# Low-part products last in each branch column tile, and a larger readiness margin for two early steps of a hybrid attention and retention layer

## The chip, the cores and the metric

The kernel runs on one core of a Trainium2 chip. The metric is the device time of one execution in microseconds (us); the times below are medians of several executions. The engines are named as in the profile: PE is TensorE (matmuls; PEld its weight loads), DVE is VectorE, ACT is ScalarE, POOL is GpSimd, and SP is the queue that issues the DMAs of this kernel. A trailing q (PEq) means the engine's sequencer.

## The reference

One layer of a streaming encoder is applied to 2048 new frames (the prompt) and to 64 frames of a running stream (the sample), which has 4096 frames of cached keys and values.

```
h = rmsnorm(x, norm_g) @ w_in            # 1024 -> 6144 columns
qa, ka, va, za, qb, kb, vb, zb, ga, gb = split(h)
qa, ka = rmsnorm over each 64 of qa, ka  # 4 heads, two 64-wide halves
oa = softmax(q0 k0) v - lam * softmax(q1 k1) v    # differential attention, ALiBi, chunk mask
ob = retention(qb, kb, vb)                        # per-head decay, chunks of 64
oa = rmsnorm(oa) * 0.8 * silu(za)
ob = rmsnorm(ob) * silu(zb)
m = sigmoid(ga) * (oa @ w_oa) + sigmoid(gb) * (ob @ w_ob)
y = x + m @ w_out
```

The outputs are y, the normalised keys, the values and the retention states, for the prompt and for the sample. All is float32. TensorE is given operands in a reduced float32 type, so each operand is split into a high part (rounded) and a low part (what is left), and a product is three matmuls: high by high, high by low and low by high.

## The kernel before, in words

**One order for all engines, written by a planner.** The program is unrolled in Python. TensorE, ACT and DVE carry out their instructions in just the order in which the generator writes them (their schedule is manual). That order comes from a list scheduler in the kernel itself: class Hybrid keeps a clock for each engine (`self.pe`, `self.act`, `self.dve`, `self.pool`, `self.dma`); P, A, V and G (L258 to L272) add the cost that the planner assumes for one instruction and return the time when its result is taken to be there (250 ns behind its end). Work is cut into generator tasks with priorities. A task yields the planner time at which it wants to go on; `loop` (L197) resumes the task of the best priority whose time has come on TensorE's clock, and if there is none, moves that clock forward. So a `yield t` puts other tasks' matmuls ahead of what follows; what is written then waits on the chip by semaphores for its true inputs. Two margins that are added to such times matter here: SLACK is 400 ns and LAND is 2000 ns.

**Stages.** First the prompt's first 1024 rows and the sample's 64 rows go through the input projection (wide pieces of 512 columns, `natural`, then Strassen-like products, `strassen`), and beside them the sample's attention runs (`sample_attn`, `sample_pv`). Then the second 1024 rows are scaled and split (`x_scaled`, `x_split`, L494 and L540) and projected, with the prompt's attention heads and the retention beside it. Last come the branch projections (`out_stream`, `m_tile`) and the output projection (`y_quad`).

**Key and query rows, `fin_qk` (L1289).** For each 128 rows of a key or query piece: ACT squares the PSUM bank, DVE reduces and scales, a small reciprocal root follows, DVE writes the normalised rows `raw` (L1325), the planner time t of which is given SLACK more (L1326) and yielded. Behind it come the store of the rows to the key output (keys only), four transposes on PE (L1340), the split of the result on ACT and DVE into a high and a low part (L1350 to L1356), and their stores to the DRAM scratch kT or qT. `t0` is the first row of the tile; it is 0 only for the first tile of the prompt, once for the keys and once for the queries. The buffers are `ev` (3), `tlo` (2) and `thi` (1).

**The sample's probabilities times values, `sample_pv` (L2209).** For each of 4 heads, 5 tiles of probabilities: PE transposes them (L2273) into a bank, ACT rounds (L2287) and DVE subtracts (L2289), which makes the pieces `atp`; there are two pieces per tile (one in the last), nine per head. A piece is entered in `parts` with its planner time plus 500 ns (L2291). The inner function `mms` (L2252) yields until the later of that time and of the time of the split values `vhl` (two buffers, filled by `v_split`: ACT L2186, DVE L2189), then writes four matmuls (L2258). The products of one tile are written after the transposes of the next. The heads' result is folded at L2135; `x_scaled` waits for it.

**Branch column tiles, `m_tile` (L2654).** For each group g of 264 columns (256 prompt rows and 8 sample rows), branch br and column tile ct of 128 there is one accumulation over four 128-row slices kt of the branch width. `self.wo[br][kp]` holds the weights' high and low parts (wh, wl), and `og[kp]` the gated branch's (ogh, ogl), two slices in one tile; `og_fin` (L2609) makes them, ogh on ACT (L2627) and ogl on DVE (L2630), and enters them with 700 ns of margin. For each kt three matmuls are written: wh by the high part (L2673), wh by the low part (L2674), wl by the high part (L2675). `m_fin` (L2681) then multiplies the bank by the gate on DVE (L2686) and adds the branches (L2698).

Of the kernel before, what the change touches and what calls it, by code (L numbers as in the profile page):

```python
# [27 lines left out]
GW = 264  # L28
# [12 lines left out]
SLACK = 400.0  # L41
PACE = 700.0
LATE = 1000.0
LAND = 2000.0
# [128 lines left out]
class Hybrid:  # L173
# [1115 lines left out]
    def fin_qk(self, which, g, nh=2):  # L1289
        nc = self.nc  # L1290
        ep = self.ep
        hs = slice(2 * g, 2 * g + nh)

        def fin(ps, r, nu, t0, t, bank="mm"):
            n, ng, rt = 128 * nh * nu, 2 * nh * nu, r * nu
            yield from self.take("ev")
            yield from self.take("tlo")
            raw = self.sb(ep, [128, 512], "ev", "raw")[:r, :n]
            sq = self.sb(ep, [128, 512], "tlo", "sq")[:r, :n]
            ms = self.sp.tile([128, 8], F32, tag="ms", name="ms")[:r, :ng]  # L1300
            raw3 = raw.rearrange("p (g d) -> p g d", d=64)
            nc.scalar.activation(sq, ps, AF.Square)
            t1 = self.A(n, t)
            if which == "q":
                nc.scalar.copy(raw, ps)
                t2 = self.A(n, t)
            else:
                nc.vector.tensor_mul(raw3, ps.rearrange("p (g d) -> p g d", d=64),  # L1308
                                     self.gk[:r].unsqueeze(1).to_broadcast([r, ng, 64]))
                t2 = self.V(n, t)  # L1310
            self.give(bank, max(t1, t2))
            yield t1
            nc.vector.tensor_reduce(ms, sq.rearrange("p (g d) -> p g d", d=64),
                                    axis=AX.X, op=ALU.add)
            t = self.V(n, t1)
            self.give("tlo", t)
            if which == "q":
                nc.vector.scalar_tensor_tensor(out=ms, in0=ms, scalar=64.0 * EPS,
                                               in1=self.qinv[:r, 2 if nh == 4 else g, :ng], op0=ALU.add, op1=ALU.mult)
            else:  # L1320
                nc.vector.tensor_scalar(ms, ms, 1.0 / 64, EPS, op0=ALU.mult, op1=ALU.add)
            t = self.V(80)
            yield t
            rs = yield from self.rsqrt_small(ms, ng, t)
            nc.vector.tensor_mul(raw3, raw3, rs.unsqueeze(2).to_broadcast([r, ng, 64]))  # L1325
            t = self.V(n + 100) + SLACK  # L1326
            yield t
            ts = 0
            if which == "k":
                if t0 < T:  # L1330
                    dst = self.o["k_prompt"][0, 0, t0:t0 + rt, hs]
                else:
                    dst = self.o["k_sample"][0, 0, :, hs]
                ts = self.rows_out(dst.rearrange("t h c d -> t (h c d)"), raw, nu, nh << 16)
            yield from self.take("tp")
            tp = self.psum("tp")
            for u in range(nu):
                for h in range(nh):
                    c = 128 * (nh * u + h)
                    nc.tensor.transpose(tp[:, h * rt + u * r:h * rt + u * r + r], raw[:, c:c + 128],  # L1340
                                        self.ident[:r, :r])
                    t = self.P(256)
            self.give("ev", max(t, ts))
            yield from self.take("thi")
            yield from self.take("tlo")
            hi = self.sb(ep, [128, 512], "thi", dt=F32R)[:, :nh * rt]
            lo = self.sb(ep, [128, 512], "tlo", dt=F32R)[:, :nh * rt]
            pt = tp[:, :nh * rt]
            if which == "q":
                nc.scalar.activation(hi, pt, AF.Identity, scale=self.gq)  # L1350
                nc.vector.scalar_tensor_tensor(out=lo, in0=pt, scalar=self.gq, in1=hi.bitcast(F32),
                                               op0=ALU.mult, op1=ALU.subtract)
                dst = self.qT
            else:
                nc.scalar.copy(hi, pt)
                nc.vector.tensor_sub(lo, pt, hi.bitcast(F32))  # L1356
                dst = self.kT
            t1 = self.A(n, t, 40)
            t2 = self.V(n, t1)
            self.give("tp", t2)  # L1360
            for d, s, tag, w in zip(dst, (hi, lo), ("thi", "tlo"), (t1, t2)):
                if w > self.pe:
                    yield w
                self.give(tag, self.st(d[hs, :, t0:t0 + rt].rearrange("h p t -> p h t"),
                                       s.bitcast(F32).rearrange("p (h t) -> p h t", h=nh), nh * nu << 16))
            if t0 == T:
                self.fresh.add(which)

        return fin
# [839 lines left out]
    def sample_pv(self, h, units, tail, tt, te, lp, oall, moved):  # L2209
# [3 lines left out]
        nc = self.nc  # L2213
# [8 lines left out]
        for _ in range(3):  # L2222
            t = self.V(9, te[-1])
        yield t
        yield from self.take("s")
        ps = self.psum("s")
        nc.tensor.matmul(ps[:, 0:2], self.fold, l, start=True, stop=True)
        t = self.P(512)
# [5 lines left out]
        for _ in range(3):  # L2234
            t = self.V(100, t)
# [30 lines left out]
        for m in range(5):  # L2266
            nt, r = (4, 128) if m < 4 else (1, 64)
            yield tb[m // 2]
            yield from self.take("at")
            at = self.psum("at")  # L2270
            for k in range(nt):
                src = units[m // 2][:, (m % 2) * 512 + 128 * k:(m % 2) * 512 + 128 * k + 128] if m < 4 else tt
                nc.tensor.transpose(at[:r, r * k:r * k + r], src, self.ident[:r, :r])  # L2273
                t = self.P(256)
            if m == 1 or m == 3:
                self.drop(units[m // 2], t)
            tags = ("ath", "atl") if m < 4 else ("ath",)
            if todo is not None and not self.has(*tags):
                yield from mms(*todo)
                todo = None  # L2280
            parts = []
            for k, tag in enumerate(tags):
                yield from self.take(tag)
                a = self.sb(ap, [128, 512], tag, "atp", F32R)
                c = at[:r, :128 * nt].rearrange("p (k c q) -> p k c q", c=2, q=64)[:, :, k]
                s = a[:r, :128 * nt].rearrange("p (k c q) -> p k c q", c=2, q=64)
                nc.scalar.copy(s[:, :, 0], c)  # L2287
                t2 = self.A(64 * nt, t)
                nc.vector.tensor_sub(s[:, :, 1], c, s[:, :, 0].bitcast(F32))  # L2289
                t2 = self.V(64 * nt, t2)  # L2290
                parts.append((a, tag, t2 + 500))  # L2291
            self.give("at", t2)
            yield self.pe
            if todo is not None:
                yield from mms(*todo)
            todo = (m, nt, r, parts)
        yield from mms(*todo)
        t = done[0]
        yield t
        oh = oall[:, 128 * h:128 * h + 128]  # L2300
        nc.scalar.activation(oh, pv[:, 0:128], AF.Identity, scale=num)
        t = self.A(128, t, 90)
# [351 lines left out]
    def m_tile(self, g, br, ct, second, og):  # L2654
        nc = self.nc
        csl = slice(128 * ct, 128 * ct + 128)
        self.nbank += 1
        tag = ("mm", "s", "at", "mm", "s", "at", "pv", "tp")[self.nbank % 8]
        yield from self.take(tag)
        ps = self.psum(tag)[:, :GW]  # L2660
        for kt in range(4):
            kp, u = divmod(kt, 2)
            wh, wl, tw = self.wo[br][kp]
            yield lambda: ct // 2 in tw
            ready = tw[ct // 2]
            if u == 0 and len(og) == kp:
                yield lambda: self.ogs[g, br, kp]
                og.append(self.ogs[g, br, kp][0])
                ready = max(ready, og[-1][2])
            if ready > self.pe:  # L2670
                yield ready
            oh, ol = (o[:, GW * u:GW * u + GW] for o in og[kp][:2])
            nc.tensor.matmul(ps, wh[:, u, csl], oh, start=kt == 0, stop=False)  # L2673
            nc.tensor.matmul(ps, wh[:, u, csl], ol, start=False, stop=False)  # L2674
            nc.tensor.matmul(ps, wl[:, u, csl], oh, start=False, stop=kt == 3)  # L2675
            for _ in range(3):
                t = self.P(GW)
        self.spawn(self.m_fin(g, br, ct, second, ps, tag, t), 0)
        yield self.pe

# [526 lines left out]
```

## Time and profile before

| what | value |
|---|---|
| median of 3 runs | 1882.4 us (1882.38 to 1887.38) |
| profiled execution, its own time | 1886.05 us |
| span of the profiled execution | 1883.4 us |
| instructions in it | 33013 |
| granted TensorE clock | 1.0 throughout |
| DMA moved | 340.07 MB, mean 181 GB/s |

The span runs from the first to the last instruction of one execution; the difference to its own time lies before and after. In the list of waits a row names the instruction that waited, who released it, the total in us, the number of times and the longest. In a timeline row stand the start and the duration in us, the engine, the line, the operation, the tiles (out<-in), the shape, a count where like instructions are merged (the duration then reaches from the first start to the last end), and in square brackets the engine's idle time before it and who ended it. A matmul's duration is modelled and longer than the step from one matmul to the next, since they are pipelined; steps are read from start to start. In the view of a line or a tile a row has the shortest, median and longest duration in ns and the first and last start in us.

### The profile page before, as it was taken

To read this page: it belongs to the slowest core of one execution; us is meant where nothing else is said; L and a number is where in the kernel's file an instruction comes from. 1 tells how busy PE (TensorE), PEld (TensorE's weight loads), DVE (VectorE), ACT (ScalarE), POOL (GpSimd) and SP (SyncE) were. 2 spreads that over 40 slices of the span, in tenths; PEclk is the share of its full clock that TensorE was granted. 3 is DMA by queue.
4 is the path that set the end of the run, shared out by engine and by line. 5 is a ranking of instruction groups with operands and counts; after the bars stand their busy time and mean duration, and the time that the engine had idled before them with its cause. 6 is when DMAs were issued, how large, how long until landed. Compare 5 with 4: busy or idle time off the path is not lost.

```text
span 1883.4 us, 33013 instructions
## 1 busy us (share of the span) xinstructions
PE 1866.8 (99%) x11090; PEld 1644.6 (87%) x11090; DVE 1328.1 (71%) x3112; ACT 975.3 (52%) x2266; POOL 678.6 (36%) x728
## 2 busy tenths in 40 slices
PE   9999999999999999999999999999999999999999
PEld 7788878888888789888988889899999999998887
DVE  6765856658585678787587877777876769887664
ACT  6444545554434566555455655556666446654221
POOL 2420366555552122122210344253224555532442
PEclk9999999999999999999999999999999999999999
DMA  7654555666767967565523659446437988886552
GB/s 255 216 175 123 161 166 169 176 200 198 240 189 186 253 198 190 152 174 169 145 72 101 172 136 238 129 123 154 126 109 234 259 250 255 263 257 211 165 157 78
DMA packets 402555, 340.07 MB, mean 181 GB/s; under 512 B 85329, under 2 KB 348625, under 8 KB 401362
## 3 DMA queue, kind: packets, MB, share of 16 engines
q1 hardware_dynamic: 402386, 337.97, 61.8%
q8 instruction: 87, 1.43, 0.3%
q14 instruction: 82, 0.67, 0.1%
HBM read 218.27 MB, written 118.75 MB: 179 GB/s over the span
## 4 chain that ended last, share of the span: by engine, by line
PE 82%; DMA 7%; DVE 5%; ACT 2%; SPq 2%; issue 1%; POOL 1%; DVEq 0%; ACTq 0%; POOLq 0%
PE mm L1137 27%; PE mm L989 8%; PE tp L989 4%; PE at L1992 3%; PE s L1880 2%; PE s L1881 2%; PE s L989 2%; PE pv L1972 2%; PE pv L1971 2%; PE pv L1970 2%; DMA ws<-in_w_in_dram 2%; PE s L2799 1%; PE s L2798 1%; PE s L2797 1%; SPq L280 1%
## 5 line engine op out<-in xcount | busy, mean ns | idle before, releaser
L748 POOL TENSOR_TENSOR wl<-ws,wh 128x512 fp32r<-128x512 f32 x107 | 148.9, 1402 | 256.4 <-ACT wh L727 181.5
L1137 PE MATMUL mm<-wh,xh 128*128 128x512 f32 x504 | 203.0, 403 | 0.0
L1137 PE MATMUL mm<-wh,xl 128*128 128x512 f32 x504 | 198.2, 393 | 0.0
L1137 PE MATMUL mm<-wl,xh 128*128 128x512 f32 x504 | 198.0, 393 | 0.1
L1137 PE MATMUL mm<-xh,wh 128*128 128x288 f32 (+2 forms) x544 | 179.8, 330 | 0.0
L1137 PE MATMUL mm<-xh,wl 128*128 128x288 f32 (+2 forms) x544 | 175.6, 323 | 0.0
L1137 PE MATMUL mm<-xl,wh 128*128 128x288 f32 (+2 forms) x544 | 175.5, 323 | 0.0
L1920 ACT ACTIVATE row<-row,a_mx 128x1024 f32<-128x1024 f32 (+7 forms) x144 | 149.8, 1042 | 11.9 <-DVE a_mx L1899 11.9
L2008 DVE TENSOR_TENSOR atl<-at,ath 128x512 fp32r<-128x512 f32 (+1 forms) x144 | 92.6, 658 | 76.6 <-ACT ath L2006 76.3
L2006 ACT CAST ath<-at 128x512 fp32r<-128x512 f32 (+1 forms) x144 | 79.1, 564 | 106.6 <-PE at L1992 106.0
L856 POOL TENSOR_TENSOR wl<-ws,wh 128x256 fp32r<-128x256 f32 x64 | 54.8, 856 | 199.0 <-ACT wh L847 198.9
L1747 POOL TENSOR_TENSOR r_y<-r_y,r_sq 128x256 f32<-128x256 f32 x32 | 28.3, 884 | 238.2 <-DVE r_sq L1744 154.5
L1137 PEld LDWEIGHTS mm<-wh,xl 128*128 128x128 f32 x504 | 94.6, 188 | 21.5
L1137 PEld LDWEIGHTS mm<-wl,xh 128*128 128x128 f32 x504 | 95.0, 188 | 18.5 <-POOL wl L748 0.9
L1137 PEld LDWEIGHTS mm<-wh,xh 128*128 128x128 f32 x504 | 94.8, 188 | 17.8 <-DVE raw L1308 0.2
L1137 PEld LDWEIGHTS mm<-xh,wh 128*128 128x128 f32 x544 | 102.4, 188 | 7.2
L1137 PEld LDWEIGHTS mm<-xl,wh 128*128 128x128 f32 x544 | 102.5, 188 | 6.9
L1137 PEld LDWEIGHTS mm<-xh,wl 128*128 128x128 f32 x544 | 102.3, 188 | 6.6
L1889 DVE CUSTOM_DVE_ANT_0 row<-s,dfar 128x512 f32<-128x512 f32 (+2 forms) x141 | 87.1, 629 | 23.8 <-PE s L1881 18.0
L1942 DVE SCALAR_TENSOR_TENSOR row<-row,a_w 128x1024 f32<-128x1024 f32 (+5 forms) x88 | 96.9, 1106 | 0.0
L1880 PE MATMUL s<-K,q 128*128 128x512 f32 (+3 forms) x240 | 90.5, 378 | 1.2 <-DVE a_acc L1889 1.2
L727 ACT CAST wh<-ws 128x512 fp32r<-128x512 f32 x111 | 67.7, 620 | 41.4 <-DMA ws<-in_w_in_dram 12.7
(543 smaller groups left out, 6075.4 us busy)
## 6 DMA issues: line engine op xcount, KB each, us to landing
ws<-in_w_in_dram SPq DMA_DIRECT2D x155, 256.0 KB, 3.5
q<-qT SPq DMA_DIRECT2D x128, 128.0 KB, 3.9
K<-kT SPq DMA_DIRECT2D x48, 256.0 KB, 4.7
V<-vN SPq DMA_DIRECT2D x24, 512.0 KB, 5.9
row<-in_x_prompt_dram SPq DMA_DIRECT2D x16, 512.0 KB, 4.6
wz<-in_w_in_dram SPq DMA_DIRECT2D x32, 256.0 KB, 4.3
row<-in_cache_k_T_dram SPq DMA_DIRECT2D x32, 256.0 KB, 3.2
row<-in_cache_v_diff_dram SPq DMA_DIRECT2D x32, 256.0 KB, 3.8
```

What stands on the lines that cost most here:

```text
L727: self.nc.scalar.copy(h, st)
L748: eng.tensor_sub(l, st, h.bitcast(F32))
L856: nc.gpsimd.tensor_sub(l[:, cs], src, h[:, cs].bitcast(F32))
L989: nc.tensor.matmul(ps, w[:, c], xs[x][c], start=bool(tag) and c == 0 and i == 0, stop=c == 3 and i == 2, skip_group_check=True)
L1137: nc.tensor.matmul(ps, p, q, start=c == 0 and i == 0, stop=c == KC - 1 and i == 2)
L1880: nc.tensor.matmul(ps, q1s, kk, start=True, stop=False)
L1889: nc.vector.tensor_tensor_reduce(out=row[:, k0:k0 + n], in0=ps, in1=tab, scale=-SLOPES[h], scalar=3.0e38, op0=ALU.add, op1=ALU.min, accum_ ...
L1920: nc.scalar.activation(u, u, AF.Exp, bias=mx, scale=-1.0, accum_out=lp[:, k:k + 1])
L1942: nc.vector.scalar_tensor_tensor(out=u0, in0=u1, scalar=w[:, 0:1], in1=u0, op0=ALU.mult, op1=ALU.add)
L1992: nc.tensor.transpose(at[:, w:w + 128], src, self.ident)
L2006: nc.scalar.copy(ah[:, :w], at[:, :w])
L2008: nc.vector.tensor_sub(al[:, :w], at[:, :w], ah[:, :w].bitcast(F32))
```

## The change

Three places are edited. In `fin_qk` the margin behind the normalised rows becomes LAND (2000 ns) in place of SLACK (400 ns) for the tile with t0 == 0. In `sample_pv` the margin of each piece becomes LAND in place of 500 ns. In `m_tile` the twelve matmuls of a tile are written in another order: for each kt the two products with the high part of the gated branch, and after all four kt the four products with its low part; the last of these now closes the accumulation. The number of matmuls and their operands stay the same.

```diff
@@ -1323,7 +1323,7 @@
             yield t
             rs = yield from self.rsqrt_small(ms, ng, t)
             nc.vector.tensor_mul(raw3, raw3, rs.unsqueeze(2).to_broadcast([r, ng, 64]))
-            t = self.V(n + 100) + SLACK
+            t = self.V(n + 100) + (LAND if t0 == 0 else SLACK)
             yield t
             ts = 0
             if which == "k":
@@ -2288,7 +2288,7 @@
                 t2 = self.A(64 * nt, t)
                 nc.vector.tensor_sub(s[:, :, 1], c, s[:, :, 0].bitcast(F32))
                 t2 = self.V(64 * nt, t2)
-                parts.append((a, tag, t2 + 500))
+                parts.append((a, tag, t2 + LAND))
             self.give("at", t2)
             yield self.pe
             if todo is not None:
@@ -2669,12 +2669,16 @@
                 ready = max(ready, og[-1][2])
             if ready > self.pe:
                 yield ready
-            oh, ol = (o[:, GW * u:GW * u + GW] for o in og[kp][:2])
+            oh = og[kp][0][:, GW * u:GW * u + GW]
             nc.tensor.matmul(ps, wh[:, u, csl], oh, start=kt == 0, stop=False)
-            nc.tensor.matmul(ps, wh[:, u, csl], ol, start=False, stop=False)
-            nc.tensor.matmul(ps, wl[:, u, csl], oh, start=False, stop=kt == 3)
-            for _ in range(3):
-                t = self.P(GW)
+            nc.tensor.matmul(ps, wl[:, u, csl], oh, start=False, stop=False)
+            for _ in range(2):
+                self.P(GW)
+        for kt in range(4):
+            kp, u = divmod(kt, 2)
+            nc.tensor.matmul(ps, self.wo[br][kp][0][:, u, csl], og[kp][1][:, GW * u:GW * u + GW],
+                             start=False, stop=kt == 3)
+            t = self.P(GW)
         self.spawn(self.m_fin(g, br, ct, second, ps, tag, t), 0)
         yield self.pe
```

## The prediction

> **What bounds the kernel now.** I began with the page's busy times, went on to the list of who TensorE waited for, and from there to the timeline around the three places that the change touches.
>
> ```profile
> span 1883.4 us, 33013 instructions
> ...
> PE 1866.8 (99%) x11090; PEld 1644.6 (87%) x11090; DVE 1328.1 (71%) x3112; ACT 975.3 (52%) x2266; POOL 678.6 (36%) x728
> ```
> ```profile
> PE at L2674 <- DVE ogl L2630: 1.9, 4, 1.0
> PE pv L1970 <- ACT ath L2006: 1.6, 1, 1.6
> PE tp L1880 <- DMA q<-qT: 1.4, 1, 1.4
> PE s L1880 <- DVE a_acc L1889: 1.2, 1, 1.2
> PE tp L1340 <- DVE raw L1325: 1.1, 1, 1.1
> ...
> PE pv L2258 <- DVE atp L2289: 0.9, 1, 0.9
> ```
>
> TensorE sets the end: 1883.4 - 1866.8 = 16.6 us are left in which it does not work, and no instruction of it is added or taken away by this change. So a gain can only come out of those 16.6 us (and the slower restart behind a wait, which counts as busy), while a loss has no such ceiling. Three of the six waits shown stand at lines that the change touches: 1.9 at L2674 (branch tiles), 1.1 at L1340 (transposes of a key tile), 0.9 at L2258 (the sample's probabilities times values): 3.9 us. The other three are in places that the edits do not name.
>
> **The first key tile.** The 400 ns of margin become 2000, so 1.6 us more in the planner's clock before the four transposes are written into TensorE's order.
>
> ```profile
> 82.77 0.40 PE L1137 MATMUL mm<-wl,xh 128*128 128x512 f32 x1
> 83.01 0.40 PE L1137 MATMUL mm<-wh,xl 128*128 128x512 f32 x1
> 84.50 0.66 PE L1340 MATMUL tp<-ident,raw 128*128 128x128 f32 x4 [1.09 <-DVE raw L1325]
> ```
> ```profile
> 83.75 0.69 DVE L1325 TENSOR_TENSOR raw<-raw,sm_y 128x512 f32<-128x512 f32 x1
> ```
>
> A projection matmul of 512 columns starts 0.24 us after the one before (82.77, 83.01), so the transposes could have started at 83.25 and started at 84.50: 1.25 us lost, of which 1.09 is plain idling. A projection yields after every six matmuls, 1.4 us; 1.6 us of margin moves the transposes by one or two such groups, to 84.7 or 86.1, when the tile (ready at 83.75 + 0.69 = 84.44) is there. Gain 1.2 (1.1 to 1.3). Moved with them: the store of the key tile on the SP queue, the ACT copy and the DVE subtraction that split it, and the two stores of the parts. The second key tile takes the next of three evacuation buffers, and its matmuls are what TensorE runs meanwhile; were no buffer free, it would wait at most the same 1.6 us. The stored parts are read back only by the attention heads, a stage later. The first query tile moves alike: only one wait is listed at L1340, so there is nothing to gain there and, with projections behind it, nothing to lose.
>
> **The sample's weights.** The margin on each split piece of the transposed probabilities grows from 500 to 2000 ns: 1.5 us in 36 pieces (nine per head).
>
> ```profile
> 280.32 0.40 PE L989 MATMUL mm<-S1h,wl 128*128 128x512 f32 x1
> 281.64 1.60 PE L2258 MATMUL pv<-vhl,atp 128*128 128x256 f32 x8 [0.92 <-DVE atp L2289]
> ...
> 289.77 1.14 PE L2258 MATMUL pv<-vhl,atp 128*128 128x256 f32 x8
> ```
> ```profile
> 432.55 1.61 PE L2258 MATMUL pv<-vhl,atp 128*128 128x256 f32 x8
> ```
> ```profile
> 281.18 0.41 DVE L2289 TENSOR_TENSOR atp<-at,atp 128x256 fp32r<-128x256 f32 x1
> 282.02 0.42 DVE L2289 TENSOR_TENSOR atp<-at,atp 128x256 fp32r<-128x256 f32 x1 [0.44 <-ACT atp L2287]
> 282.90 0.42 DVE L2289 TENSOR_TENSOR atp<-at,atp 128x256 fp32r<-128x256 f32 x1 [0.46 <-ACT atp L2287]
> ...
> 288.27 1.84 DVE L2189 TENSOR_TENSOR vhl<-row,vhl 128x512 fp32r<-128x512 f32 x2
> ```
>
> The first piece was ready at 281.59 and used at 281.64: 281.64 - (280.32 + 0.24) = 1.08 us lost. The eight matmuls of its first two pieces then took 1.60 where an unhindered eight took 1.14: 0.46 more; the same eight in another head took 1.61: 0.47. Sum 2.0, lower bound the 0.9 of the wait list. With 1.5 us more, six projection matmuls fit in between. I take 1.8 (0.9 to 2.0), near the top, since the readiness of both pieces falls inside the new margin. What this does to the sample's own chain: the third piece was ready at 282.90 + 0.42 = 283.32 and used only at 289.77, directly behind the split of its values (288.27 to 290.11 for two). So past the first two pieces the values decide, not the pieces, and the larger margin is hidden by them: a head is late by about 1.5 us, not nine times that, and four heads by at most 6 us. The loads of later values on the SP queue and their splits on ACT and DVE, released by the products, slip by the same 1.5. Behind the sample wait the scaling of the next 1024 rows and their splits:
>
> ```profile
> L2135 PE MATMUL pv<-fold,row x8: 218/275/275, 528.0 to 528.8; 128*128 128x64 f32 x8
> ```
> ```profile
> L528 DVE SCALAR_TENSOR_TENSOR row<-row,gT,rb x24: 472/953/1058, 544.7 to 566.2; 128x256 f32<-128x256 f32 x24
> ```
> ```profile
> L561 ACT CAST xh<-xT x4: 620/622/625, 580.0 to 582.1; 128x512 fp32r<-128x512 f32 x4
> ```
>
> The scaling ends at 566.2 + 0.95 = 567.2; the first split, which needs the first half's input tiles to be done with, starts at 580.0. That is 12.8 us of cover for at most 6 us of delay, so I cost it at nothing.
>
> **The branch tiles.** Twelve matmuls each, 16 tiles in 8 groups, in a new order: eight that need only the high part of the gated branch, then the four that need its low part. Whether a step changes weights or not shows no difference:
>
> ```profile
> 1557.65 0.39 PE L2674 MATMUL at<-ogl,w_o_diffh 128*128 128x264 f32 x1 [0.98 <-DVE ogl L2630]
> ...
> 1558.01 0.28 PE L2673 MATMUL at<-ogh,w_o_diffh 128*128 128x264 f32 x1
> 1558.12 0.28 PE L2674 MATMUL at<-ogl,w_o_diffh 128*128 128x264 f32 x1
> 1558.25 0.28 PE L2675 MATMUL at<-ogh,w_o_diffl 128*128 128x264 f32 x1
> 1558.37 0.28 PE L2673 MATMUL at<-ogh,w_o_diffh 128*128 128x264 f32 x1
> ...
> 1559.10 0.28 PE L2673 MATMUL pv<-ogh,w_o_diffh 128*128 128x264 f32 x1
> ```
> ```profile
> 1580.84 0.29 PE L2673 MATMUL at<-ogh,w_o_reth 128*128 128x264 f32 x1
> ...
> 1582.28 0.39 PE L2674 MATMUL at<-ogl,w_o_reth 128*128 128x264 f32 x1 [0.42 <-DVE ogl L2630]
> ...
> 1582.99 0.28 PE L2673 MATMUL pv<-ogh,w_o_reth 128*128 128x264 f32 x1
> ```
> ```profile
> 1628.75 0.40 PE L2674 MATMUL at<-ogl,w_o_reth 128*128 128x264 f32 x1 [0.37 <-DVE ogl L2630]
> ...
> 1629.90 0.39 PE L2674 MATMUL at<-ogl,w_o_reth 128*128 128x264 f32 x1 [0.16 <-DVE ogl L2630]
> ...
> 1630.61 0.29 PE L2673 MATMUL pv<-ogh,w_o_reth 128*128 128x264 f32 x1
> ```
> ```profile
> 1556.91 1.31 DVE L2630 TENSOR_TENSOR ogl<-on,ogh 128x528 fp32r<-128x528 f32 x2
> ...
> 1578.65 3.57 DVE L2630 TENSOR_TENSOR ogl<-on,ogh 128x528 fp32r<-128x528 f32 x2
> ...
> 1626.86 2.98 DVE L2630 TENSOR_TENSOR ogl<-on,ogh 128x528 fp32r<-128x528 f32 x2
> ```
>
> The steps are 0.11 (same weights again), 0.13 and 0.12 (new ones): 0.121 us. A difference of 5 ns in the 512 pairs that lose their neighbour would be 2.6 us either way; I take 0. Now the three groups in which TensorE waited, with the two low parts of each landing as the DVE rows say. First: the wait stood ahead of the second product, so the tile began 0.98 + 0.28 earlier, at 1556.39. The low products are then due at 1556.39 + 8 x 0.121 = 1557.36 and start at 1557.65 as the first part lands; the second part's, due at 1557.89, start at 1556.91 + 1.31 + 0.05 = 1558.27, and the next tile at 1558.51 instead of 1559.10: 0.59 gained. Second: seven products ran from 1580.84 and the second part (1578.65 + 3.57 = 1582.22) was late; its products are now due at 1582.05 and start at 1582.27, the next tile at 1582.51 for 1582.99: 0.48. Third: begun at 1628.75 - 0.37 - 0.28 = 1628.10; second part at 1626.86 + 2.98 = 1629.84, its products at 1629.90, next tile 1630.14 for 1630.61: 0.47. Sum 1.5. Were nothing left of the waits (next tile at its start + 12 x 0.121), 1.26 + 0.70 + 1.06 = 3.0. From below, the second high part is needed two products earlier, 0.24 us in each of three groups: 0.8. I take 1.5, which the rows give. The reading of the finished bank by DVE comes behind the last product as before.
>
> The three places give 1.2 + 1.8 + 1.5 = 4.5 us (2.8 to 6.3, before the 2.6 either way of the steps). The profiled execution took 1886.05 around its 1883.4 of span, 3.65 above the median of the runs, 1882.4; with the same order of instructions in each, I take the sum off both: 1881.5 for a profiled one and **1877.9** for the median.
>
> **The rivals.** *Taken back elsewhere*: the planner writes one order for all engines; moving wake-ups at 84 us shifts every later choice. The rows of waits that the change does not name (1.6, 1.4, 1.2: 4.2 us) show how large such accidents are. If as much comes anew, 1882.4. For it: those waits sit at places with the same margins; against: over 1700 us the order left only these. *More than the sum*: the same accidents vanish: 1877.9 - 4.2 = 1873.7. *The low parts no longer late at all*: the pair of subtractions took 1.31 us in the first group and 3.57 in the second, when GpSimd was at work:
>
> ```profile
> 1578.33 1.60 POOL L2613 TENSOR_TENSOR on<-on,z 128x528 f32<-128x528 f32 x1 [0.23 <-DMA on<-oaT]
> 1579.88 1.78 POOL L2539 TENSOR_TENSOR wt43l<-wst,wt43h 128x512 fp32r<-128x512 f32 x1
> ```
>
> A shifted order that parts the two engines gives 3.0 rather than 1.5: 1876.4. Against: nothing in the edit moves GpSimd against DVE. The Trainium skill (GPSIMD Engine Reference, section Specifications) says that GpSimd's SBUF interface is shared with VectorE for instructions with two SBUF inputs; the rows agree. *The sample too late* (slower): should the 1.5 us be paid at each of the 20 tiles of probabilities, not once a head, the chain slips 30 us; past the 12.8 of cover TensorE stands at the start of the second half for 17.2: 1882.4 - 4.5 + 17.2 = 1895.1. It decides from nine tiles on (13.5 us). Against it stands the wait of 6.4 us for values that the third piece shows. The Trainium skill (TensorE: Matmul & The Clock Gate, Part 1) adds that an idle window of some 3.4 us halves the clock; by it this case would be about 1.7 us worse, and no row here idles that long.
>
> **How the numbers follow.** Forecast 0.50 (own range 1876.0 to 1880.5), taken back 0.27 (1880.5 to 1887), more than the sum 0.12, low parts 0.05, sample too late 0.06. A measurement here tells about 0.3%, 5.6 us, from no change: faster means below 1876.8, slower above 1888.0. Below lie 0.12, a quarter of the forecast and half of the low-part case: 0.27. Above lie 0.06 and a tail of 0.03 of taken back: 0.09. Within: 0.64. The range from 1873.0 to 1886.5 leaves out the slow case, that tail and part of the fast one.
>
> **What would show it.** Right: no idle ahead of L1340 near 84 us, eight matmuls at L2258 in 1.1 us in every head, the low products still held in two or three groups, by under 0.6 us each. Wrong: new waits of TensorE over 1 us between 100 and 660 us, the sample's end past 535 us, a step in the branch tiles other than 0.121, or splits of the second half that start later than 580 for want of scaled rows.

## The result, and the profile after

The changed kernel took 1887.8 us, the median of 20 executions; two of them, over 2500 us at a granted clock near 0.67, were disturbed, and the median of the other 18 (1884.25 to 1892.52) is 1887.2. The kernel before, on the same chip, took 1883.25. The ratio is 1.002 with a 95% interval of 1.0014 to 1.0027: slower by 0.2%, about 4 us, where 1877.9 was forecast.

The head of the page and the first rows of the list of who TensorE waited for, of the changed kernel:

```profile
span 1884.6 us, 32992 instructions
...
PE 1867.7 (99%) x11090; PEld 1647.2 (87%) x11090; DVE 1334.7 (71%) x3112; ACT 975.9 (52%) x2266; POOL 668.0 (35%) x728
```
```profile
PE mm L1137 <- ACT wh L727: 1.7, 1, 1.7
PE s L1566 <- DVE ev L1586: 1.3, 1, 1.3
PE pv L1970 <- ACT ath L2006: 1.2, 1, 1.2
...
PE pv L2410 <- DVE row L2404: 1.0, 1, 1.0
PE mm L1137 <- DVE raw L1308: 0.9, 1, 0.9
PE mm L1137 <- POOL wl L748: 0.9, 1, 0.9
PE mm L1137 <- ACT raw L1305: 0.7, 1, 0.7
...
PE at L2679 <- DVE ogl L2630: 0.6, 1, 0.6
```

The rows of L1340 and L2258 are gone and that of the low products is down from 1.9 to 0.6: the two named waits of the margins were taken away and most of the third, as intended. Of the rows that stand here instead, all but the one of L1970 (1.6 before) and the rest of the low products' are new, and they stand at lines that no edit touches.

The key tile, in TensorE's and DVE's timelines of the changed kernel:

```profile
83.06 0.40 PE L1137 MATMUL mm<-wh,xl 128*128 128x512 f32 x1
84.32 0.50 PE L1137 MATMUL mm<-wh,xh 128*128 128x512 f32 x1 [0.86 <-DVE raw L1308]
...
85.81 0.60 PE L1340 MATMUL tp<-ident,raw 128*128 128x128 f32 x4
```
```profile
78.96 3.50 DVE L881 TENSOR_TENSOR row<-xh,xl 128x512 f32<-128x512 f32 x2
...
82.97 0.69 DVE L1325 TENSOR_TENSOR raw<-raw,sm_y 128x512 f32<-128x512 f32 x1
83.58 0.68 DVE L1308 TENSOR_TENSOR raw<-mm,gk 128x512 f32<-128x512 f32 x1
```

The transposes no longer wait, but the projection tile that now goes ahead of them does. It needs the PSUM bank that DVE's L1308 empties, and L1308 stands right behind L1325 in DVE's order, behind the same two long additions (3.50 us). What was late is DVE; the wait only changed its place, from 1.09 to 0.86 us. It is there in every kernel below with a margin of 1800 or 2000 ns on the key tile, at 0.8 to 1.5 us.

The sample. First its first products (L2258), then its end (L2135, 528.0 before) and the scaling of the second half's rows (L528, 544.7 to 566.2 before):

```profile
294.21 1.12 PE L2258 MATMUL pv<-vhl,atp 128*128 128x256 f32 x8
```
```profile
L2135 PE MATMUL pv<-fold,row x8: 218/275/275, 545.0 to 545.8; 128*128 128x64 f32 x8
```
```profile
L528 DVE SCALAR_TENSOR_TENSOR row<-row,gT,rb x24: 468/473/1521, 561.6 to 591.3; 128x256 f32<-128x256 f32 x24
```

Eight products in 1.12 us, as forecast (and so in each of the four heads), but at 294.21 and not 281.64, and the sample ends 17 us later, not 6.

### The profile page after: what moved, and what is told of

It reads as the page before. It is cut to its first block, busy times and chain, and to the rows that moved or that the text cites. A ratio compares the mean times of both kernels' runs of the same rounds, so it can differ in the third digit from the quotient of the medians.

```text
span 1884.6 us, 32992 instructions
## 1 busy us (share of the span) xinstructions
PE 1867.7 (99%) x11090; PEld 1647.2 (87%) x11090; DVE 1334.7 (71%) x3112; ACT 975.9 (52%) x2266; POOL 668.0 (35%) x728
## 4 chain that ended last, share of the span: by engine, by line
PE 90%; DVE 3%; DMA 3%; ACT 1%; SPq 1%; issue 1%; POOL 1%; ACTq 0%; DVEq 0%; POOLq 0%
PE mm L1137 29%; PE mm L989 9%; PE tp L989 5%; PE at L1992 3%; PE s L1881 2%; PE s L1880 2%; PE s L989 2%; PE pv L1972 2%; PE pv L1971 2%; PE pv L1970 2%; PE s L2803 1%; PE s L2802 1%; PE s L2801 1%; PE mm L1566 1%; DMA ws<-wsum 1%
```

## Why the sample ends 17 us later: a race for two buffers

ACT's timeline between two heads of the sample shows it: L2095 copies the next head's keys, L2287 rounds this head's probabilities. Before:

```profile
423.27 1.14 ACT L2095 CAST ath<-row 128x512 fp32r<-128x512 f32 x2
429.43 0.37 ACT L2287 CAST atp<-at 128x256 fp32r<-128x256 f32 x1 [3.40 <-PE s L2057]
```

After:

```profile
432.56 0.37 ACT L2287 CAST atp<-at 128x256 fp32r<-128x256 f32 x1 [2.65 <-PE at L2273]
...
443.62 0.61 ACT L2095 CAST ath<-row 128x512 fp32r<-128x512 f32 x1
```

Both use the buffers `ath` and `atl`, two of each. Before, the last head's first two key pieces took them at 423 us, so its scores ran on beside the previous head's products. After, the previous head's probabilities took them first, and the keys came at 443.6. The planner settles this once, by the two tasks' times in its own clock: with the times of before the keys go first by 0.7 us (419.29 against 419.97); a margin of 2000 ns on the pieces alone makes it the other way round by 1.0 us (427.98 against 427.02). These four are times in us that the planner's own clock shows when the program is generated, not times on the chip. The key margin alone gets there by way of an earlier head: on the chip head 1's keys come at 281 us instead of 297, and the last head's at 451. So a delay is not passed on as it is. With 1600 ns on the key tile the sample ends 0.9 us later than with the products alone, with 1800 ns, where the race is turned, 19 us later; how much a turn costs differs from kernel to kernel, as the next table shows.

## The experiments

Times are medians over 7 to 12 executions (the 18 undisturbed ones for the change); "against before" is the median less that of the kernel before on the same chip (1881.8 to 1883.6). The end of the sample is the first start at L2135 in the profile. The order is how TensorE's some 6000 matmuls between 600 and 1527 us stand in the trace, by source line and tile. It falls into three kinds: within the first and within the second, 99.2% or more of the sequence agrees, between them 44%; the third agrees with either to about half.

| kernel | sample ends | order | median us | against before | ratio, 95% interval |
|---|---|---|---|---|---|
| before | 528.0 | first | | 0 | |
| the change | 545.0 | second | 1887.2 | +4.0 | 1.0014 to 1.0027 |
| key margin alone | 545.0 | second | 1888.5 | +4.9 | 1.0016 to 1.0035 |
| sample margin alone | 547.0 | second | 1889.7 | +6.1 | 1.0020 to 1.0045 |
| products alone | 525.8 | first | 1881.7 | -1.9 | 0.9984 to 1.0001 |
| products, key margin | 544.8 | second | 1887.6 | +4.1 | 1.0011 to 1.0032 |
| products, key 1600 ns | 526.7 | first | 1882.0 | -0.9 | 0.9987 to 1.0005 |
| products, key 1800 ns | 544.8 | second | 1887.8 | +4.9 | 1.0015 to 1.0037 |
| the change, sample 2500 ns | 530.5 | first | 1880.4 | -2.6 | 0.9978 to 0.9995 |
| products, key 1600, sample 1300 | 528.1 | first | 1880.6 | -2.3 | 0.9977 to 0.9994 |
| products, keys held 3 us | 534.2 | first | 1879.2 | -3.6 | 0.9979 to 0.9996 |
| products, keys held 20 us | 544.3 | second | 1887.9 | +5.0 | 1.0012 to 1.0032 |
| the change, head 2 held 3 us | 535.5 | first | 1880.4 | -2.5 | 0.9982 to 1.0000 |
| products, rows held 17 us | 526.2 | first | 1883.8 | +0.9 | 0.9992 to 1.0011 |
| the change, last rows unpaced | 544.9 | third | 1889.1 | +5.6 | 1.0020 to 1.0044 |
| products, opening held 6 us | 526.1 | second | 1885.2 | +1.6 | 0.9990 to 1.0014 |
| the change, rows paced wider | 545.1 | first | 1883.0 | +1.2 | 0.9996 to 1.0014 |

**Parts of the change.** The first four take one or two of its three edits, in the lines of the diff shown above.

> Only the margin of the first key and query tile. Theory A (each edit acts where it stands): the wait of 1.1 us near 84 us goes, but the one of 0.9 us ahead of the next projection tile stays as in the changed kernel, so within 0.5 us of the kernel before. Theory B (the edit rewrites the order of all that follows): a difference of 2 us or more, of either sign, from waits between 100 and 700 us that have no link to the key tile; the end of the sample's attention moves by more than 3 us from 528.8.

> Only the larger margin of the sample's weights. Theory A: eight products per head without a wait, 1.8 us faster, the sample's end at 530 to 535 us. Theory B: the keys of the next head take the buffers ahead of the products, the sample's end slips to 540 us or later, the projection weights of the second half come late and TensorE idles 2 us or more between 590 and 640 us: 2 to 5 us slower than before.

> Only the new order of the products in the branch tiles. Both theories: nothing changes ahead of 1520 us; the waits at the low-part products fall from 1.9 us to under 1.0; 1.0 to 2.0 us faster. A rival, that each product costs a few ns more in the new order: the step from product to product is over 0.122 us and the kernel is 1 us or more slower.

> The change without the sample's margin. Theory A: 1.5 us faster (products) and no more. Theory B, with the sample's margin as the only cause of the late second half: the waits and the half clock between 612 and 626 us of the changed kernel are absent, and it is not slower than before. If it is as slow as the changed kernel (about 4 us), the key tile's margin is the cause.

The product order gains 1.9 us and its profile lists no wait at the low products at all. Either margin alone loses, and by as much as both: the two losses do not add. That fits a switch, and no sum of displaced pieces.

**The switch, by small steps of a margin.** In the first two only the first tile's margin differs from the products alone (1800.0 in the second), in the third only the pieces' margin from the whole change; the fourth has the products, 1600.0 and 1300.

```diff
@@ fin_qk @@
-            t = self.V(n + 100) + SLACK
+            t = self.V(n + 100) + (1600.0 if t0 == 0 else SLACK)
@@ sample_pv, the whole change @@
-                parts.append((a, tag, t2 + LAND))
+                parts.append((a, tag, t2 + LAND + 500))
```

> Low products last and the first tile's ready time 1600 ns after DVE's multiply (400 before, 2000 in the change); the sample's margin as before. Theory A, the flipped hand-over: the loss comes when the margin of the first tile pushes the planner over a point where head 3's first keys of the sample get their buffers after head 2's probability pieces instead of before them; 1600 stays short of that point, so the sample's last value products (L2135's normalising steps) stay near 528 us and the time is that of the products alone, about 1881 to 1882 (1880 if the wait of 1.1 us at L1340 is truly gone). Theory B, the displaced work: later transposes put the root chain and the copies of DVE and ACT behind other work, whatever the sample does, and nearly all of the 1200 ns more in the margin's 1600 is there already; it expects the time of the two edits together, 1886 to 1889, with the sample where it was.

> The same with 1800 ns, 200 ns more than the run before it. Theory A: the other side of the point: head 3's first key copies near 445 to 451 us instead of 423, the sample's end near 545 us instead of 528, and 1886 to 1889 us, 5 us or more above the kernel with 1600. Theory B: 200 ns more of the same displacement, so at most 1 us from the kernel with 1600, in either sense.

> The whole change, but the pieces of the sample's weights get 2500 ns in place of 2000. Theory A: the larger margin falls back on the early side of the hand-over: head 3's first keys near 425 us, the sample's end near 530 us, and a time of 1879 to 1883, so more of the change's own edit takes the loss away. Theory B, by which a later piece costs more the later it is: 1888 to 1891, with the sample's end past 545 us.

> Low products last, 1600 ns for the first tile and 1300 ns for the sample's pieces (500 before): both waits that the change aims at are at most 1.1 us, so these margins cover most of them, and the hand-over stays early. Theory A: the sample's end by 532 us, and the products' gain plus what the two waits are worth where they do not come back, 1878 to 1882. Theory B: as the whole change, 1886 to 1889.

200 ns between 1600 and 1800 cost 5.8 us and move the sample's end by 18. And 500 ns more of the margin that had lost 6.1 alone make the whole change faster than before: at 2500 ns the race is won again. Displaced work (theory B) does not fit: a cost of lateness would not be taken away by more lateness.

**The race alone, without a margin.** In the first two, the last head's first key piece is held back in the planner, and both margins are those of before; in the third, the whole change stands and the other side of the race is held back.

```diff
@@ sample_attn, products alone (20000 in the second) @@
+                if h == 3 and m == 0:
+                    yield self.pe + 3000
                 if todo is not None and not self.has("ath", "atl"):
@@ sample_pv, the whole change @@
-            yield tb[m // 2]
+            yield tb[m // 2] + (3000 if h == 2 and m == 0 else 0)
```

> Low products last and neither margin changed; the planner holds head 3's first key piece back by 3 us of its TensorE clock, so that head 2's probability pieces take the two buffers first. Theory A (the order of the hand-over and how late the sample ends set the time): head 3's first key copy moves from 421 to some 440 us, the sample's end from 526 to 533 to 540, and the time goes from the products' 1881.7 to 1883 to 1887, with no ready time touched. Theory B (the two later ready times cost by themselves): no ready time is later, so 1881 to 1883.

> The same with the piece held back by 20 us. Theory A: the sample's end near 545 us, as in the whole change, waits of TensorE for the second half's weights at 615 to 622 us, and 1886 to 1889. Theory B: 1881 to 1883, since both margins are those of before. A third possibility, that late ends alone are harmless and that the later first tile and a late end have to come together: within 1 us of the products' 1881.7 although the sample ends near 545.

> The whole change with both its margins, and head 2's first probability transposes due 3 us later, so that head 3's first keys take the buffers before them. Theory A: head 3's first key copy near 430 us instead of 444, the sample's end near 533 to 536 instead of 545, and 1880 to 1884 against the change's 1888. Theory B: nothing that the change made later is taken back and one more piece is late, so 1888 or more.

The second and third came as theory A has it: without either margin the change's loss, and with both margins the gain. The first is a miss that teaches: the keys lost the race there too, the sample ended at 534.2, 8 us later than with the products alone, and the kernel was the fastest of all. So neither the lost race nor some lateness costs in itself. Between 535.5 and 544.3 something else turns.

**What turns behind the sample.** The attention memory of the second half opens once all of its scaled rows are split, and with it the loads for the prompt's attention heads begin. Three kernels vary that step: the scaling held, the last scalings not overtaken by splits, and the opening held.

```diff
@@ x_scaled, products alone @@
         yield lambda: len(self.rooted) >= 8 and self.n_spv == 5
+        yield self.pe + 17000
@@ x_scaled, the whole change @@
-                    yield self.dve - PACE
+                    if p < 3:
+                        yield self.dve - PACE
@@ attn_zone, products alone @@
-        yield self.marks["half0"]
+        yield max(self.marks["half0"], self.pe + 6000)
```

> Low products last and neither margin changed; the sample's heads run as in that kernel (its end near 526 us) but the scaling of the second half's rows, which waits for the sample's end, is held for 17 us more, about the slip that the change made. Theory A1 (the sample's end costs because the scaling of the second half's rows starts late): first scalings at L528 near 551 to 554 us instead of 535, the last ones past 588, the first loads of the second half's attention (dnear, K) issued near 597 instead of 592, TensorE waiting for a weight split at 615 to 622 us, and 1886 to 1889. Theory A2 (a late sample costs through what it holds itself, its memory, its TensorE work moved to after 530 us, the buffers of the hand-over): scaling late but 1881 to 1883.5, and no wait for weights near 620.

> The whole change, but the eight scalings of the last pair of row tiles are issued in one go instead of one by one, so that the splits of the earlier pairs do not come between them on DVE. Theory A3 (the opening of the second half's attention memory, which waits for the last split of the scaled rows, sets the time): the sample still ends near 545 us, but the last scaling comes near 580 us instead of 591, the first load behind the opening (dnear) near 591 to 593 instead of 597.9, no wait for weights near 620, and the time falls from 1887.8 to 1880 to 1884. Rival (the late sample costs by itself, the opening is only a sign): 1886 to 1889.

> Low products last, neither margin changed, and only the opening of the second half's attention memory held for 6 us of the planner's clock. Theory A3: the sample's end stays near 526 us and the splits stay where they were, dnear is issued near 597 to 599 us instead of 592.3, and the time rises from the products' 1881.7 to 1886 to 1889. Rival: 1881 to 1883.5.

The held scaling gave 1883.8, just above the range of theory A2 and far from that of A1. It lost 2.8 us against the products alone. A wait of TensorE of 1.92 us up to 532.25 us (0.4 us at that line in the other kernels that list it) and a granted clock of 0.50 from 533.5 to 536.9 us behind it could account for that; whether late rows cost anything besides is open. The opening as a moment (theory A3) fell. The first load behind it in the SP queue's timeline, after the change, with the last rows unpaced, and with the opening held:

```profile
597.90 0.37 SPq L280 DMA_DIRECT2D dnear<-in_c_dnear_dram  x1
```
```profile
592.28 0.33 SPq L280 DMA_DIRECT2D dnear<-in_c_dnear_dram  x1
```
```profile
592.50 0.33 SPq L280 DMA_DIRECT2D dnear<-in_c_dnear_dram  x1
```

With the last rows unpaced it went out as early as with the products alone (592.26), and the time was 1889.1. With the opening held it went out early too, at 592.50 and not at 597 to 599 as was expected, so this run does not test the moment. Yet the time rose by 3.5 us above the products alone, and later waits of the change (at L2371 and L2410) appeared although the sample had ended at 526. That pointed to the order of the second half, and so the traces were compared as sequences. The column "order" is the outcome: no kernel with the first order is above +1.2, and none with another is below +1.6. (These two, the last kernel and the held opening, are not told apart by their intervals; the others are, for the most part.) Where the first two orders part is plain in the timeline, in the place of the first score product of the prompt's attention. With the products alone, then after the change, then with the opening held:

```profile
602.14 0.22 PE L1880 MATMUL s<-K,q 128*128 128x128 f32 x1
602.93 0.30 PE L1881 MATMUL s<-K,q 128*128 128x128 f32 x1 [0.57 <-DMA q<-qT]
```
```profile
609.62 0.22 PE L1880 MATMUL s<-K,q 128*128 128x128 f32 x1
```
```profile
608.77 0.22 PE L1880 MATMUL s<-K,q 128*128 128x128 f32 x1
```

The first attention head is put in later, and from there on the orders part: with the opening held, TensorE's matmuls are those of the kernel before up to this place.

**Late sample, first order.** The last kernel is the whole change with another pace of the scalings, chosen since its plan keeps the late sample and has the first order behind it.

```diff
@@ x_scaled, the whole change @@
-                    yield self.dve - PACE
+                    yield self.dve - 4 * PACE
```

> The whole change, but each scaling of the second half's rows may be issued 2.8 us before DVE is free in the planner's clock instead of 0.7 us; the plan then keeps the late sample (its end near 545 us) and has TensorE's order of the kernel before from 600 us on. Theory A4 (the second half's order of work costs): the waits of the change at 620, 808, 1123 and 1304 us are gone, those of the kernel before at 615 (L1880) and 1195 us (L1880) are back, and the time is 1880 to 1884, with at most the 2 us that TensorE loses between 540 and 600 us above the products' 1881.7. Rival (the late sample costs whatever order follows): 1886 to 1889.

It came out at 1883.0 with the sample's end at 545.1, inside the 1880 to 1884 of theory A4 and outside the rival's range. But the kernel before took 1881.8 on this chip, so it lies 3.1 us above the products alone where theory A4 allowed 2: the first order takes away about half of the loss, not all of it. Its own list of waits has the rows of the first order again:

```profile
PE s L1880 <- DVE a_acc L1889: 1.3, 1, 1.3
PE s L2673 <- DVE ga L2690: 1.1, 1, 1.1
PE pv L1970 <- ACT ath L2006: 1.1, 1, 1.1
PE tp L1880 <- DMA q<-qT: 1.1, 1, 1.1
```

Together with the held opening this makes a square, each cell against the products alone (-1.9): late sample in the first order +3.1, early sample in the second order +3.5, both +5.9 to +6.9 (the change and three kernels like it). The two halves add up to 6.6; each single one is uncertain by about 2 us, as the intervals show.

What the second order loses shows in TensorE's busy time by windows (start and end, length, then busy time of PE, PEld, DVE, ACT and POOL, granted clock, DMA share, GB/s). Products alone, the last kernel, the change, the held opening:

```profile
600.00:1450.00 850.00, 844.90 (x5454) 766.10 (x5453) 621.47 (x1755) 499.89 (x1141) 233.94 (x292) 1.00 0.57 160
1450.00:1720.00 270.00, 269.88 (x2159) 267.84 (x2158) 213.68 (x375) 144.45 (x340) 125.10 (x98) 1.00 0.84 250
```
```profile
600.00:1450.00 850.00, 844.70 (x5452) 765.99 (x5451) 620.60 (x1757) 499.77 (x1141) 232.94 (x291) 1.00 0.57 160
1450.00:1720.00 270.00, 268.86 (x2157) 267.29 (x2157) 213.70 (x373) 144.06 (x339) 126.37 (x99) 1.00 0.84 250
```
```profile
600.00:1450.00 850.00, 843.74 (x5431) 764.57 (x5430) 627.79 (x1753) 499.97 (x1138) 228.18 (x292) 1.00 0.58 160
1450.00:1720.00 270.00, 267.09 (x2152) 265.46 (x2151) 214.98 (x372) 142.06 (x337) 122.95 (x97) 1.00 0.83 244
```
```profile
600.00:1450.00 850.00, 845.89 (x5458) 766.66 (x5457) 629.60 (x1758) 501.00 (x1142) 227.87 (x292) 1.00 0.58 160
1450.00:1720.00 270.00, 265.19 (x2130) 263.07 (x2129) 210.47 (x368) 140.76 (x336) 121.90 (x96) 1.00 0.82 241
```

The idle time over the 1120 us is 5.2 and 6.4 us in the first order (5.10 + 0.12; 5.30 + 1.14), 9.2 and 8.9 in the second (6.26 + 2.91; 4.11 + 4.81). Over all kernels that have the products last it is 4.4 to 8.2 us in the eight with the first order, 8.6 to 9.6 in the five with the second and 9.4 in the one with the third. The kinds do not overlap, but the range within the first is wider than the gap. It is not the same wait in both: the change idles ahead of weights near 620 us, the held opening at the low products near 1582, where it lists 2.4 us. What of it belongs to the plan and what to the one execution that was profiled stays open. So does what the late sample costs with the first order behind it: its idle time is only 1.2 us above that of the products alone.

## Why the prediction was wrong, point by point

**What failed.** The step is the sentence on the sample's chain: the larger margin "is hidden by them: a head is late by about 1.5 us, not nine times that, and four heads by at most 6 us", costed at nothing under 12.8 us of cover. The argument that values and not pieces set the pace of a head held where no race turned: with the sample margin alone the last products of the first two heads start 0.3 us later than before (312.5 for 312.2, 395.0 for 394.7). And the first split after the change came even earlier than before (577.7 us, not 580.0). But the delay went into a race between two tasks for the same buffers, and the sample ended 17 us late. The paragraph on the key tile failed at the same place: it has no way from that tile to the sample, and the key margin alone ends the sample at 545.0 and costs 4.9 us. The cover was also measured at the first split, while it is the last one that opens the next stage, and the scalings, late by 17 us, now shared DVE with the first splits and dragged on to 591.3. Neither the rows held alone (+2.8 against the products alone, in part by the hold's own wait) nor the moment of the opening explains a loss of some 6 us. About half of it goes with the planner's answer, another order from 600 us on (+3.5); the other half comes with the late sample (+3.1), and by what way is not shown.

**The rivals.** The loss is that of "taken back elsewhere": moved wake-ups shift every later choice. It was given 0.27 and the price of the waits that stood in the profile, 4.2 us (1877.9 + 4.2 is 1882.1; the 1882.4 that is written there takes back the whole 4.5); the runs show 1887.8 - 1877.9 = 9.9. "The sample too late" saw the right place, but by another mechanism (1.5 us paid on each tile, TensorE standing still at the start of the second half). Two of the prediction's own signs for a wrong forecast are there: the sample's end past 535 us, and a new wait over 1 us at 619.6.

**The products.** 1.5 us was forecast; 1.9 was measured alone, with an interval that reaches from a gain of 3 us to none. The step is 0.122 us, where 0.121 was taken. After the change one group still waits, where two or three were expected to:

```profile
1582.90 0.52 PE L2679 MATMUL at<-ogl,w_o_reth 128*128 128x264 f32 x2
1584.05 0.51 PE L2679 MATMUL at<-ogl,w_o_reth 128*128 128x264 f32 x2 [0.64 <-DVE ogl L2630]
```

**The two margins were worth less than their waits.** The forecast took 1.2 and 1.8 us from rows of one execution. TensorE's order up to 500 us is the same in the kernel before and in the products alone (2300 matmuls compared one by one; it goes on being the same up to 1527 us), so the same waits should be there if they belonged to the order. They are not; the products alone show:

```profile
83.66 0.66 PE L1340 MATMUL tp<-ident,raw 128*128 128x128 f32 x4 [0.23 <-DVE raw L1325]
279.75 1.26 PE L2258 MATMUL pv<-vhl,atp 128*128 128x256 f32 x8
```

Of 1.09 us at L1340, 0.23 is left, and at L2258 no wait is listed. Among the other kernels with this order up to there, with the opening held it is 0.68 and none, with the keys held 3 us 1.06 and none. The two waits come and go with the execution, and the step "I take the sum off both", the profiled time and the median, was wrong with them. With the first order kept, the whole change (head 2 held, or 2500 ns) is at -2.5 and -2.6 against -1.9 for the products alone: by the medians the margins are worth some 0.6 us and not 3.0, and the intervals, over 1.5 us either way, do not tell that from nothing.

## What to carry to other kernels

Where a planner writes one order for all engines, a margin can throw a switch and not only delay. Before costing it, look for two tasks that take the same buffers within a microsecond of each other, and compare the traces of two plans as sequences before comparing their waits. A wait that is read from one execution is worth its mean over several; look for it in a second execution of the same order before it goes into a sum. To test a change of this kind, vary its number in both directions: a loss that goes away with 1600 ns on the key tile, and again with 2500 ns on the pieces, is not the price of the margin, and products last with 1600 and 1300 ns, or the whole change with 2500, keeps its gain and is faster than both kernels.

## What was not expected of the hardware

Behind the new waits of the changed kernel near 620 us TensorE ran at half speed for a while. Its timeline, and the window of 10 us around it (the number behind the last bracket is the granted clock):

```profile
617.55 0.39 PE L1137 MATMUL mm<-wh,xl 128*128 128x512 f32 x1
619.61 0.49 PE L1137 MATMUL mm<-wh,xh 128*128 128x512 f32 x1 [1.67 <-ACT wh L727]
620.96 0.50 PE L1137 MATMUL mm<-wl,xh 128*128 128x512 f32 x1 [0.86 <-POOL wl L748]
...
623.09 0.63 PE L1137 MATMUL mm<-wh,xl 128*128 128x512 f32 x1
623.52 0.63 PE L1137 MATMUL mm<-wh,xh 128*128 128x512 f32 x1
623.95 0.63 PE L1137 MATMUL mm<-wl,xh 128*128 128x512 f32 x1
```
```profile
616.00:626.00 10.00, 7.47 (x27) 5.48 (x26) 4.76 (x17) 4.10 (x10) 1.27 (x1) 0.83 0.91 278
```

The steps are 0.43 us instead of 0.23, and the granted clock of the window is 0.83, though no single wait was longer than 1.67 us: two waits with one matmul between them went ahead of it. In the kernel with the rows held, the clock was 0.50 from 533.5 to 536.9 us behind a single wait of 1.92 us. The same pair of waits near 620 us gave 0.66 in the same window with the keys held 20 us, and 1.00 with the products and the key margin. The Trainium skill (TensorE: Matmul & The Clock Gate, Part 1) has the clock halved after an idle window of some 3.4 us, and says that this window runs freely, so that one kernel has a different number of slow matmuls at its start from run to run. The traces fit the second also in the middle of a kernel, with 0.83, 0.66 and 1.00 behind the same pair of waits in three kernels of one order; as to the first, TensorE was not idle for 3.4 us without a break in any of these places. The prediction had read the rule as asking for one idle stretch of that length. The clock was not what told the kernels with the loss from those with the gain: in five kernels with the first order the granted clock from 612 to 624 us was 0.86, and with the products and the key margin it was 1.00.
